# A 256 MB rotation by 90 degrees: the SBUF side of a DMA described as two runs of 8 KB instead of one of 16 KB

## The chip, the cores and the metric

The kernel runs on one core of one Trainium2 chip. The metric is device time in microseconds (us): 1260.99 us is the median of three runs before the change (1260.99 to 1261.13). The core has a tensor engine (PE), a vector engine (DVE), a scalar engine (ACT), GpSimd (POOL) and a sync engine (SP), and 16 DMA engines that move data between its on-chip memory (SBUF, 128 partitions) and the chip's main memory (DRAM).

## The reference

```python
def setup_inputs():
    return {"x": np.random.randn(8192, 8192).astype(np.float32), "k": 1}

def reference(x, k):
    return np.rot90(x, k)
```

With k = 1, `out[i, j] = x[j, 8191 - i]`: a transpose with the order of the columns reversed. Nothing is computed; 268 MB are read and 268 MB written.

## The kernel before

**Tiling.** The input is cut into 16 macros of 1024 rows (R) by 4096 columns (W). A macro comes in as 8 loads (T), each of 128 rows by 4096 columns: one row of 16 KB for each of the 128 partitions, 2 MB in all. It goes out as 8 stores (J), each of 512 input columns by 1024 input rows: 512 output rows of 1024 elements. In SBUF a store's buffer holds, for each partition, four output rows (G = 4) of 4 KB one behind the other, so 16 KB without a hole; in DRAM these four rows lie far apart. Two stores of the last macro are shaped otherwise: eight rows of 2 KB for each partition (END = 4 row blocks instead of 8).

**Stages.** There are 128 loads and 128 stores, 2 MB each.

1. SP issues load m into one of the landing buffers (LAND = 2 of them once the kernel runs; at the start the three output buffers take loads as well). It waits until the buffer's last load was read (`taken`, line 176).
2. DVE copies or transposes what landed into `ring` (line 337), an SBUF array that holds one macro. The slots that load m writes are those that output n = m - 8 was made from, so DVE first waits until output n is made (`s_pool` or `s_half`).
3. Output n is made in one of OUTS = 3 output buffers, either by PE (transposes into PSUM, line 376) with ACT copying from PSUM (line 415), or, for the outputs that DVE transposed in 32 by 32 blocks, by moves of these blocks on POOL (line 294, nine of sixteen), ACT (line 405, six) and DVE (line 319, one). In the macros between the first and the last ones, outputs 0 and 4 are made by PE and the other six by moves. Whoever writes an output buffer waits until the last store from it has landed (`room_for`, line 167).
4. ACT issues the store of output n (line 425).

So loads and stores hold each other: a load's rows can only go into `ring` when the output eight places before it is made, and an output can only be made when a store has given its buffer back.

**Queues.** Loads lie in SP's DMA queue (q1 in the profile), stores in ACT's (q10). Both run on the same 16 DMA engines. Each transfer has 128 partitions; each DMA engine takes eight of them.

**The place of the change.** `whole_reads` (line 37) goes through the finished program and rewrites the source pattern of some DMAs. A pattern is a list of (step, count) pairs, in elements, with the partitions first. The rewrite applies where the source has three such pairs, the last one contiguous, and the middle step as long as the last run:

- a load's source is `x[r0 + ..., c0 : c0 + W]`, which has two pairs, (8192, 128) and (1, 4096): the condition is not met;
- a store's source is the output buffer seen as `"m (g f) -> m g f"`: (4096, 128), (1024, 4), (1, 1024), or (4096, 128), (512, 8), (1, 512) for the two of the last macro. Here it is met, for all 128 stores.

Before the change it turns a store's source into (4096, 128), (1, 1), (1, 4096), one run of 16 KB for each partition. The destination stays as it was: four runs of 4 KB (or eight of 2 KB) for each partition.

Of the kernel before, what the change touches and what calls it, by code (L numbers as in the profile page):

```python
# [11 lines left out]
W = 4096  # L12
# [24 lines left out]
def whole_reads(nc):  # L37

    for fn in nc.m.functions:
        for block in fn.blocks:  # L40
            for n, ins in enumerate(block.instructions):
                if not isinstance(ins, mybir.InstDMACopy):
                    continue
                src = ins.ins[0]
                ap = [list(d) for d in src.ap]
                if len(ap) == 3 and ap[2][0] == 1 and ap[1][0] == ap[2][1]:
                    ap = [ap[0], [1, 1], [1, ap[1][1] * ap[2][1]]]
                    block.instructions[n] = copy.replace(
                        ins,
                        ins=[copy.replace(src, ap=ap)],  # L50
                        ant_dge_precooked=False,
                    )
# [7 lines left out]
def kernel(tc: tile.TileContext, x: bass.AP, k: bass.AP, out: bass.AP):  # L60
    nc = tc.nc
    assert k == 1, f"only k=1 supported, got {k}"
    nc.at_finalize(whole_reads)

    N, M = x.shape
# [400 lines left out]
```

## Time and profile before

| | before |
|---|---|
| median of three runs | 1260.99 us |
| the profiled execution, time | 1261.2 us |
| its span, first to last instruction | 1259.3 us |
| data moved | 537.22 MB, mean 427 GB/s |
| busy share of the span: PE, DVE, ACT, POOL | 26%, 49%, 54%, 64% |
| queue q1 (loads): records, share of 16 engines | 18432, 50.0% |
| queue q10 (stores): records, share of 16 engines | 18432, 50.1% |
| a load, median from issue to landing | 15.3 us |
| a store, median from issue to landing | 18.6 us |

The span is the time from the first to the last instruction of one profiled execution; the time of that execution is 1.9 us longer. Line numbers are those of the kernel above. "DMA" in a list of waits means that an instruction waited for a transfer to land. The trace also has one record for each DMA packet, with its queue, start, duration and bytes: 128 records of 16 KB and 16 of 4 bytes for each load and each store, the 4-byte ones being the increments of the semaphore, one on each engine. For a store the 16 KB are what is read from one partition in one run, whatever the runs on the DRAM side.

### The profile page before, as it was taken

What the parts mean: (1) busy time and instruction counts of PE and PEld (TensorE: products, weight loads), DVE (VectorE), ACT (ScalarE), POOL (GpSimd) and SP (SyncE); (2) the same over time, 40 slices, a digit from 0 to 9 for tenths busy, and PEclk for the clock granted to TensorE, in tenths of its full rate; (3) what the DMA queues carried; (4) which work ended last, traced back from release to release, by engine and by line L of the source; (5) the groups of instructions that cost most, each with busy time, mean ns of one, the idle gap of its engine ahead of it and who ended that gap; (6) DMA issues with size and microseconds to landing.
All of it is one profiled execution on the core that took longest, in us unless ns stands there. A gap on an engine that the chain in (4) does not pass through costs nothing.

```text
span 1259.3 us, 5455 instructions
## 1 busy us (share of the span) xinstructions
PE 326.2 (26%) x1556; PEld 265.3 (21%) x1556; DVE 618.3 (49%) x373; ACT 680.7 (54%) x636; POOL 809.8 (64%) x735
## 2 busy tenths in 40 slices
PE   1555111221123211222202222022221122214373
PEld 1444011211112110121201212012120121103373
DVE  3434654555545555555555555555545554454210
ACT  0344565565556655555555555556555665556464
POOL 0001886768867679676797767977678776795500
PEclk9986555555555555555555555556555565556687
DMA  9999999999999999999999999999999999999998
GB/s 398 413 429 431 428 428 430 429 431 429 429 430 429 430 428 429 430 429 431 428 429 432 426 430 429 429 431 428 431 430 428 430 429 429 429 428 429 431 423 372
DMA packets 36893, 537.22 MB, mean 427 GB/s; under 512 B 4096, under 2 KB 4096, under 8 KB 4096
## 3 DMA queue, kind: packets, MB, share of 16 engines
q10 hardware_dynamic: 18432, 268.44, 50.1%
q1 hardware_dynamic: 18432, 268.44, 50.0%
q8 instruction: 12, 0.20, 0.1%
q14 instruction: 17, 0.14, 0.0%
HBM read 268.44 MB, written 268.44 MB: 426 GB/s over the span
## 4 chain that ended last, share of the span: by engine, by line
DMA 49%; POOL 44%; ACT 3%; issue 2%; DVE 0%; PE 0%; ACTq 0%; POOLq 0%; SPq 0%; DVEq 0%
DMA out_dram<-buf 44%; POOL buf L294 44%; DMA buf<-in_x_dram 4%; ACT buf L415 3%; DVE ring L337 0%; PE ps L376 0%; ACTq L425 0%; POOLq L270 0%; SPq L256 0%; SPq L461 0%; DVEq L324 0%; SPq L118 0%
## 5 line engine op out<-in xcount | busy, mean ns | idle before, releaser
L294 POOL COPY buf<-ring 32x1024 f32<-32x1024 f32 (+1 forms) x729 | 809.1, 1110 | 379.8 <-DMA out_dram<-buf 349.8
L405 ACT COPY buf<-ring 32x1024 f32<-32x1024 f32 (+1 forms) x486 | 497.6, 1024 | 277.8 <-POOL buf L294 178.7
L376 PE MATMUL ps<-head,ring 128*128 128x128 f32 x1496 | 313.4, 381 | 914.1 <-DMA out_dram<-buf 419.2
L376 PEld LDWEIGHTS ps<-head,ring 128*128 128x128 f32 x1496 | 252.5, 198 | 974.8 <-DVE ring L337 430.2
L337 DVE COPY ring<-buf 128x1024 f32<-128x1024 f32 (+5 forms) x152 | 162.0, 1071 | 593.4 <-DMA buf<-in_x_dram 491.3
L337 DVE STREAM_TRANSPOSE ring<-buf 128x3072 f32<-128x3072 f32 (+2 forms) x125 | 357.8, 2871 | 0.0
L415 ACT COPY buf<-ps 128x2048 f32<-128x2048 f32 (+1 forms) x133 | 172.9, 1366 | 218.5 <-PE ps L376 145.4
L319 DVE COPY buf<-ring 32x1024 f32<-32x1024 f32 x81 | 108.1, 1334 | 0.0
L398 ACT COPY buf<-ps 128x512 f32<-128x512 f32 x15 | 8.8, 585 | 64.6 <-POOL buf L294 55.4
L362 PE MATMUL ps<-head,buf 128*128 128x128 f32 x60 | 15.9, 420 | 0.0
L362 PEld LDWEIGHTS ps<-head,buf 128*128 128x128 f32 x60 | 13.0, 229 | 0.0
L332 DVE COPY buf<-buf 128x512 f32<-128x512 f32 x15 | 6.4, 428 | 0.5
L389 ACT ACT_TABLE_LOAD x1 | 1.3, 1283 | 0.9 <-SPq L118 0.9
L274 POOL MEMSET head<- 128x128 f32 x1 | 0.2, 204 | 0.5 <-SPq L118 0.5
L276 POOL TENSOR_SCALAR_AFFINE_SELECT head<-head 128x128 f32<-128x128 f32 x1 | 0.3, 292 | 0.2 <-POOL head L274 0.2
L447 POOL MEMSET const-float32-0.0<- 128x1 f32 x1 | 0.1, 98 | 0.2 <-issue 0.2
L389 ACT COPY head<-head 128x1 f32<-128x1 f32 x1 | 0.2, 191 | 0.0
L447 POOL MEMSET const-uint8-127<- 128x1 uint8 x1 | 0.1, 102 | 0.0
L447 POOL MEMSET const-bfloat16-1.0<- 128x1 bf16 x1 | 0.1, 100 | 0.0
L447 POOL MEMSET const-float32-1.0<- 128x1 f32 x1 | 0.1, 98 | 0.0
## 6 DMA issues: line engine op xcount, KB each, us to landing
buf<-in_x_dram SPq DMA_DIRECT2D x128, 2048.0 KB, 15.3
out_dram<-buf ACTq DMA_DIRECT2D x128, 2048.0 KB, 18.6
```

What stands on the lines that cost most here:

```text
L276: e.affine_select(out=ident, in_=ident, compare_op=mybir.AluOpType.not_equal, fill=1.0, base=0, pattern=[[-1, P]], channel_multiplier=1,). ...
L294: i = e.tensor_copy(out=to, in_=of)
L319: i = e.tensor_copy(out=to, in_=of)
L332: e.tensor_copy(out=at(bufs[b][:], 0, [[CH, 1], [1, CH]]), in_=landed(b, js)).then_inc(s_rev, 1)
L337: turn(out=chunk(kk, t, js), in_=landed(b, js)).then_inc(s_rev, 1)
L362: i = e.transpose(corner[:, g * P : g * P + P], bufs[load_buf(m)][:, g * P : g * P + P], ident,)
L376: i = e.transpose(ps[h][:, to : to + P], chunk(kk, t, [j])[:, 0, off : off + P], ident,)
L389: e.copy(scratch, ident[:, :1])
L398: e.copy(at(bufs[b][:], rows - P, [[rows, G], [1, P]]), at(corner, 0, [[P, G], [1, P]]),).then_inc(s_freed, 1)
L405: i = e.copy(to, of)
L415: e.copy(at(bufs[b][:], cols[0], [[rows, deep], [1, run]]), at(ps[h][:], 0, [[run, deep], [1, run]]),).then_inc(s_ev, 1)
L447: nc = _bacc.Bacc("TRN2", target_bir_lowering=False, num_devices=1)
```

## The change

One line of `whole_reads` differs. A store's source pattern becomes (4096, 128), (2048, 2), (1, 2048): two runs of 8 KB for each partition instead of one of 16 KB. The bytes, their places, the destination pattern, the order of the instructions on every engine and all waits are the same. The title under which the change was made says "of a load"; in the program it is the stores that meet the condition, and a load is described as before: one run of 16 KB on either side.

```diff
                 src = ins.ins[0]
                 ap = [list(d) for d in src.ap]
                 if len(ap) == 3 and ap[2][0] == 1 and ap[1][0] == ap[2][1]:
-                    ap = [ap[0], [1, 1], [1, ap[1][1] * ap[2][1]]]
+                    ap = [ap[0], [W // 2, 2], [1, W // 2]]
                     block.instructions[n] = copy.replace(
                         ins,
                         ins=[copy.replace(src, ap=ap)],
```

## The prediction

> **What bounds the kernel now.** I read the page's DMA part first, then its queues and its waits, then a table of windows, and last the records of single DMA packets.
>
> ```profile
> DMA  9999999999999999999999999999999999999998
> GB/s 398 413 429 431 428 428 430 429 431 429 429 430 429 430 428 429 430 429 431 428 429 432 426 430 429 429 431 428 431 430 428 430 429 429 429 428 429 431 423 372
> DMA packets 36893, 537.22 MB, mean 427 GB/s; under 512 B 4096, under 2 KB 4096, under 8 KB 4096
> q10 hardware_dynamic: 18432, 268.44, 50.1%
> q1 hardware_dynamic: 18432, 268.44, 50.0%
> buf<-in_x_dram SPq DMA_DIRECT2D x128, 2048.0 KB, 15.3
> out_dram<-buf ACTq DMA_DIRECT2D x128, 2048.0 KB, 18.6
> ```
>
> The DMA engines are full in every slice, at 429 GB/s from the third slice on; loads and stores take half each, and their shares add to 100%. Nothing lies between 512 B and 8 KB: a store is recorded as 16 KB reads although it writes runs of 4 KB.
>
> ```profile
> DVE ring L337 <- DMA buf<-in_x_dram: 491.3, 106, 8.3
> PE ps L376 <- DMA out_dram<-buf: 419.2, 21, 29.7
> POOL buf L294 <- DMA out_dram<-buf: 349.8, 29, 120.6
> ```
>
> These waits (us in total, times, longest) all end with a transfer: the engines wait for DMA. The next table gives start and end, length, the busy time of five engines, the clock, DMA share and GB/s.
>
> ```profile
> 20.00:40.00 20.00, 4.28 (x15) 2.68 (x16) 9.42 (x5) 0.00 (x0) 0.00 (x0) 1.00 1.01 431
> 100.00:1150.00 1050.00, 227.69 (x953) 181.08 (x954) 555.84 (x340) 596.43 (x572) 784.32 (x710) 0.53 1.01 429
> 1215.00:1224.00 9.00, 7.78 (x68) 7.10 (x67) 0.00 (x0) 7.76 (x6) 0.00 (x0) 1.00 1.01 417
> 1230.00:1250.00 20.00, 9.28 (x81) 8.50 (x79) 0.00 (x0) 10.90 (x6) 0.00 (x0) 0.85 1.01 428
> ```
>
> Loads alone run at 431 GB/s, both at 429, stores alone at 428, the two stores of 2 KB runs at 417: the engines are as full in each, and the rate follows how a transfer is described.
>
> The packet records say how. Laid end to end they fall into 16 engines without holes; the time from a record's start to the next one's on its engine is the price of the record. It is 607 ns for 16 KB of a load, 612 to 613 ns for 16 KB of a store, 622 ns for 16 KB of the two stores with 2 KB runs, 6 ns for the 4 bytes of a semaphore. Each engine has 128 x 8 = 1024 load records, as many store records and 256 semaphore records: 1024 x 0.607 + 1024 x 0.6125 + 256 x 0.006 = 1250.3 us. The first record starts at 2.0 us and the last ends at 1257.4 us, which leaves 5.1 us for the slower first slices (398 and 413 GB/s) and small holes. The time is this sum, so the change is worth what it does to a store record, unless it leaves the DMA engines idle.
>
> **The change part by part.**
>
> *The loads* keep their pattern: 0.
>
> *The stores' reads.* 1024 records of 16 KB on each engine become 2048 of 8 KB. The trace has no store of that form, so I bound one added record. From below: 0. The prices 607, 612.5 and 622 ns for one, four and eight written runs rise by 1.8 ns a run at first and 2.4 later; if reading and writing went on beside each other and the slower counted, four written runs (some 5 ns over the load) could already cover one more read. A gain is excluded by the rows: no 16 KB record is cheaper than 607 ns, smaller runs were dearer each time, and two 8 KB pieces carry the same bytes. From above: the program's own fetches hold records of 8 KB, of 309 ns at least, against 611 ns for a load's 16 KB (these are durations, which overlap by 3 to 4 ns): 2 x 309 - 611 = 7 ns. In between: a 4-byte record takes 6 ns, almost no data, so about 5 ns is the price of a record as such. I take 4.8 ns, because that is a record more on the same queues and engines, while the 8 KB fetches belong to another queue. The sum: 1024 x 4.8 ns = 4.9 us; from below 0, from above 1024 x 7 ns = 7.2 us. There is no cover: the engines have no holes.
>
> The Trainium skill (DMA: Bandwidth & Descriptors, "Why small descriptors are slow") puts the fixed price of a packet inside a DMA engine at about 3 cycles; at the 850 MHz that its section "Where 436 GB/s comes from" gives, an estimate is 3.5 ns, and the sum would be 3.6 us, 1264.8 us. The 6 ns of the 4-byte record agree in size.
>
> *The issue* of a store on ACT takes 547 ns, that of a load 328 ns; more read descriptors may lengthen it, by no more than the same difference, I think: 0.2 us. It costs nothing while another store is still being moved: by issue times and semaphore records there is always at least one store in flight (one in 12% of the time, two in 78%, three in 10%). Without that cover it would be 128 x 0.22 = 28 us.
>
> *The turns.* While both queues hold work, an engine's records alternate, one load record, one store record. If a turn is a record, a store now moves 8 KB in a turn against a load's 16 KB, so stores get a third of the rate while a load is in flight, not half. Bytes do not change, and loads cannot run away: DVE takes load m only when output m - 8 is made. In a steady cycle of four outputs, 39.1 us, loads would be in flight for 4 x 4.9 x 1.5 = 29 us, with stores getting 9.8 us of work meanwhile and the other 9.8 us alone: it fits exactly, provided a store is always waiting. The DVE's 491 us of waiting for loads would turn into waiting for POOL and PE. I take 0 for this; its other end is the second rival.
>
> The Trainium skill (the same page, "Queues, rings and completion order") has an engine drain a whole packet of some 9 to 17 descriptors before it changes the queue; then the shares would stay as they are. The trace disagrees: the change comes after each record.
>
> Sum: the profiled execution's 1261.2 us (span 1259.3 and 1.9 around it) stands 0.2 us above the median, so 1261.0 + 4.9 = **1265.9 us**.
>
> **The rivals.**
>
> *1. The added read is hidden in the record (not slower).* Place: inside a DMA engine, where 16 KB of a store cost 612.5 ns because of four written runs, not of the read. For it: the step from four to eight runs (2.4 ns each) is larger than that from one to four (1.8), as it would be if the first written runs hid behind something. Against: the difference is a nanosecond. Price: 0 to 1 ns a pair, so 1261.0 to 1262.0, say 1261.5 us. It decides if a pair costs under 2.4 ns more. That the two adjoining runs are put together again on the way, so that the change does nothing, gives 1261.0 and is counted here.
>
> *2. Stores lose their turns and the DMA engines run dry (much slower).* Place: POOL's wait for a store, once in a 39.1 us cycle (longest normal wait 8 us). If loads are served first, then when POOL gets its buffer back only two stores are left, 9.8 us of work, while the next output takes nine moves, 10.4 us, plus 0.55 us of issue and about 1 us to the first record: up to 2.2 us idle in each of 29 cycles, 64 us, 1325 us at most; a quarter of it, as the loads that DVE releases fill most of it, gives 1282 us. For it: the alternation by records. Against: my count of the cycle keeps a store waiting throughout, if only by 1 to 2 us. It decides where there are moments with no store in flight.
>
> *3. Loads come earlier, and that helps (faster).* The same turns shorten a load's 15.3 us; DVE and PE wait less. But the DMA engines are full, and what can be won is the 5.1 us beside the sum, most of it in the first slices, before any store: I give it 3.5 us at most, 1257.5 us, and only if the added records cost nothing.
>
> **How the numbers follow.** A measurement of this kernel can tell about 0.2%, 2.5 us, from no change. The forecast (2.5 to 7 us more) has 0.48; hidden or undone, 0.29; run dry, 0.16; faster, 0.07. So slower 0.64, same 0.29, faster 0.07. The range: the lower end 1260.5 us takes in the first rival and leaves out the third; the upper end 1280 us takes in the upper bound of the record (1268.2) and the smaller half of the second rival, and leaves out about 0.09. The likeliest case alone has 1263.5 to 1268.2 us.
>
> **What would show it.** q10 should have 128 x (256 + 16) = 34816 records, q1 its 18432 still; if q10 has 18432, the runs were joined. Two store records should cost some 617 ns together, against 612.5: at that, stores alone near the end run at 424 or 425 instead of 428 GB/s, and the middle at 427 or 428 instead of 429. If the middle stays at 429, the first rival holds. If turns go by records, a load's median falls towards 9 to 12 us, a store's rises above 19 us, and DVE's wait for loads shrinks. If digits of the DMA row fall under 9, the second rival holds. The forecast is wrong if a pair costs under 2.4 ns or over 7 ns more, or if the engines show holes.

## The result and the profile after

The changed kernel takes 1276.6 us (median of six runs, 1274.11 to 1280.41) against 1261.04 us before (six runs): a ratio of 1.0126, 95% interval 1.0107 to 1.0145. It is slower, by 15.6 us: a small change, but well clear of the scatter. The profiled execution took 1280.4 us, span 1278.5 us, so it is one of the longer ones: 19.2 us over the profiled execution of before.

The DMA part of the page of the changed kernel, with the rate of each of 40 slices, the queues (records, MB, share of 16 engines) and the issues (KB each, median us from issue to landing):

```profile
DMA  9999999999999999999999999999999999999999
GB/s 398 423 428 428 429 423 426 404 425 412 408 430 408 428 426 407 418 397 430 428 420 430 412 429 426 425 430 426 425 427 420 432 419 427 426 431 428 397 421 381
DMA packets 53277, 537.22 MB, mean 420 GB/s; under 512 B 4096, under 2 KB 4096, under 8 KB 4096
q1 hardware_dynamic: 18432, 268.44, 50.1%
q10 hardware_dynamic: 34816, 268.44, 50.0%
buf<-in_x_dram SPq DMA_DIRECT2D x128, 2048.0 KB, 12.4
out_dram<-buf ACTq DMA_DIRECT2D x128, 2048.0 KB, 20.4
```

The stores' queue has the 34816 records that two runs of 8 KB make. Loads land sooner (12.4 us, 15.3 before), stores later (20.4, 18.6 before). And the rate is no longer even: before, it was 426 to 432 GB/s from the third slice to the thirty-eighth; now slices of 430 stand beside slices of 397 to 412. The DMA row says 9 throughout all the same. A record that takes twice its time counts as busy for all of it, so this row cannot show what was lost.

The waits of the changed kernel (us in total, times, longest):

```profile
DVE ring L337 <- POOL buf L294: 392.7, 67, 9.6
POOL buf L294 <- DMA out_dram<-buf: 368.7, 58, 121.5
DVE ring L337 <- DMA buf<-in_x_dram: 166.6, 46, 8.4
```

The kernel before had this line beside the ones in the prediction:

```profile
DVE ring L337 <- POOL buf L294: 98.9, 21, 6.4
```

DVE waited 491.3 us for loads before; now 166.6 us, and 392.7 us for POOL (98.9 before): loads now lie ready and wait for the output whose place they take. POOL waits for a store 58 times instead of 29. With the landing buffers full, SP often has no load to issue: between 60 and 1190 us no load was in flight for some 5% of the time (0% before).

Windows of the changed kernel: loads alone, the middle, one bad stretch in the middle, and stores alone near the end. Columns as in the prediction's table.

```profile
20.00:40.00 20.00, 4.14 (x15) 2.55 (x16) 9.56 (x5) 0.00 (x0) 0.00 (x0) 1.00 1.01 432
100.00:1150.00 1050.00, 223.24 (x940) 179.16 (x938) 520.07 (x335) 588.38 (x565) 757.96 (x702) 0.53 1.01 422
225.00:245.00 20.00, 7.81 (x34) 7.01 (x35) 13.36 (x7) 12.90 (x12) 18.32 (x18) 0.50 1.01 399
1250.00:1270.00 20.00, 7.46 (x64) 6.92 (x64) 0.00 (x0) 9.37 (x6) 0.00 (x0) 0.84 1.01 426
```

Loads alone run as before, stores alone at 426 GB/s against 428; the loss is in the middle, 422 against 429, where both queues meet, and there in stretches like the third line.

The packet records show what happens in such a stretch. I put them end to end on their engines as for the prediction; which engine a record ran on is inferred from its start and end. On one engine, from 225 us on (L a load record of 16 KB, S a store record of 8 KB, small letters the semaphores, in brackets the ns of a record that is longer than its kind):

```
S L S L s L L l S S S S S S S S S S S S S S S S s L(1058) L L L L L L L l S S S S S S S S S S S S S S S S(534) s L(1319) L(938) S L S L S L(629) S L(725) S L S L S l
```

A load's eight records and a store's eight used to alternate, with a share of one half each. Now a store needs sixteen turns and a load still eight, so the load is through when half of the store is left; the rest of the store runs by itself, and the next load may find an engine without any store. In this line its first record then takes 1058 or 1319 ns instead of 611. Some records after it are long too, even between two stores (629 and 725 ns at the end of the line).

Three figures sum this up for each kernel of this study; none needs to know which engine a record ran on. "One side" is the share of the time, from 60 us until shortly before the last load, in which at least 14 of the 16 engines were moving for the same queue. "Long" is the time, per engine, by which records exceeded the usual length of their kind, counted where it was over 50 ns. "Idle" is the time per engine without a record. "Records" is what the records' own prices come to against before, worked out from the prices below and 1024 pieces of 16 KB per queue and engine.

| kernel (load, store records) | median us | against before | one side | long us | idle us | records us |
|---|---|---|---|---|---|---|
| before (16 KB, 16 KB) | 1261.0 | | 9.5% | 2.7 | 2.0 | 0 |
| changed (16, 8) | 1276.6 | +15.6 | 48% | 18.2 | 4.2 | -0.5 |
| e1 (8, 8) | 1267.8 | +6.7 | 6% | 1.7 | 3.5 | +4.6 |
| e2 (8, 16) | 1283.0 | +21.9 | 49% | 12.2 | 9.3 | +5.1 |
| e3 (16, 4) | 1280.3 | +19.2 | 70% | 12.6 | 3.0 | +8.7 |
| e4 (4, 4) | 1284.1 | +23.0 | 2% | 1.3 | 1.5 | +23 |
| e5 (16, 8 and 16 by turns) | 1268.9 | +7.9 | 38% | 8.3 | 1.6 | -0.3 |
| e6 (16 written as 8, 16) | 1263.5 | +2.5 | 13% | 2.3 | 2.2 | +1.5 |
| e7 (16, 16, loads held) | 1327.5 | +66.5 | 47% | 46.9 | 23.7 | 0 |
| e8 (8, 4) | 1279.8 | +18.8 | 41% | 5.4 | 1.5 | +13.8 |

"One side", "long" and "idle" are of the profiled executions (1261.2 us before, 1280.4 us for the changed kernel, 1281.9, 1282.6, 1266.5 and 1326.4 us for e2, e3, e5 and e7). For the changed kernel 15.5 us more of long records and 2.2 us more idle account for 17.7 of its 19.2 us. In every run long records, idle time and the records' own price add up to the profiled difference to within 2 us.

The prices, from a record's start to the next one's on the same engine: 607 ns for 16 KB of a load, 612 to 613 ns for 16 KB of a store, 306 ns for 8 KB of either, 155 to 156 ns for 4 KB of either. So a store's pair costs 612 ns, no more than the one record that it replaces, as far as half a nanosecond can be told here.

### The profile page after: what moved, and what is told of

Same layout as the page of the kernel before. It is cut to its first block, busy times and chain, and to the rows that moved or that the text cites. A ratio compares the mean times of both kernels' runs of the same rounds, so it can differ in the third digit from the quotient of the medians.

```text
span 1278.5 us, 5455 instructions
## 1 busy us (share of the span) xinstructions
PE 323.1 (25%) x1556; PEld 265.3 (21%) x1556; DVE 589.1 (46%) x373; ACT 680.9 (53%) x636; POOL 790.2 (62%) x735
## 2 busy tenths in 40 slices
DMA packets 53277, 537.22 MB, mean 420 GB/s; under 512 B 4096, under 2 KB 4096, under 8 KB 4096
## 3 DMA queue, kind: packets, MB, share of 16 engines
q1 hardware_dynamic: 18432, 268.44, 50.1%
q10 hardware_dynamic: 34816, 268.44, 50.0%
## 4 chain that ended last, share of the span: by engine, by line
DMA 56%; POOL 30%; ACT 8%; issue 2%; DVE 1%; PE 1%; ACTq 1%; SPq 0%; DVEq 0%
DMA out_dram<-buf 52%; POOL buf L294 30%; ACT buf L415 7%; DMA buf<-in_x_dram 4%; DVE ring L337 1%; ACT buf L405 1%; PE ps L376 1%; ACTq L425 1%; SPq L256 0%; DVE buf L319 0%; ACT buf L398 0%; DVEq L324 0%; ACTq L163 0%; SPq L461 0%; SPq L118 0%
## 5 line engine op out<-in xcount | busy, mean ns | idle before, releaser
L294 POOL COPY buf<-ring 32x1024 f32<-32x1024 f32 (+1 forms) x729 | 789.5, 1083 | 417.4 <-DMA out_dram<-buf 368.7
L405 ACT COPY buf<-ring 32x1024 f32<-32x1024 f32 (+1 forms) x486 | 497.7, 1024 | 270.3 <-DMA out_dram<-buf 178.2
L337 DVE COPY ring<-buf 128x1024 f32<-128x1024 f32 (+5 forms) x152 | 150.2, 992 | 620.8 <-POOL buf L294 392.7
L337 DVE STREAM_TRANSPOSE ring<-buf 128x3072 f32<-128x3072 f32 (+2 forms) x125 | 358.2, 2873 | 0.0
L319 DVE COPY buf<-ring 32x1024 f32<-32x1024 f32 x81 | 90.3, 1115 | 18.7 <-DMA out_dram<-buf 18.7
L362 PEld LDWEIGHTS ps<-head,buf 128*128 128x128 f32 x60 | 12.6, 224 | 0.0
## 6 DMA issues: line engine op xcount, KB each, us to landing
buf<-in_x_dram SPq DMA_DIRECT2D x128, 2048.0 KB, 12.4
out_dram<-buf ACTq DMA_DIRECT2D x128, 2048.0 KB, 20.4
```

The source lines that it names most:

```text
L294: i = e.tensor_copy(out=to, in_=of)
L319: i = e.tensor_copy(out=to, in_=of)
L337: turn(out=chunk(kk, t, js), in_=landed(b, js)).then_inc(s_rev, 1)
L362: i = e.transpose(corner[:, g * P : g * P + P], bufs[load_buf(m)][:, g * P : g * P + P], ident,)
L405: i = e.copy(to, of)
```

## The experiments

The theory after the result: an engine changes the queue after each record; where the records differ in size, the queue with the larger ones gets ahead, each queue in turn leaves the engines to the other, and records grow long in these stretches (theory of turns). The rival: each added record costs what was lost, 15 ns (theory of records). All edits are against the kernel before.

**e1: loads in two runs as well.** The loads are read and also written in two runs.

```diff
+                if len(ap) == 2 and ap[1] == [1, W]:
+                    ap = [ap[0], [W // 2, 2], [1, W // 2]]
+                    to = [to[0], [W // 2, 2], [1, W // 2]]
                 ...
-                    ap = [ap[0], [1, 1], [1, ap[1][1] * ap[2][1]]]
+                    ap = [ap[0], [W // 2, 2], [1, W // 2]]
```

> Stores read in two runs of 8 KB as in the changed kernel, and loads in two runs of 8 KB too. Theory of turns (a queue's turn is one record, and unequal turns let one queue run dry): turns are equal again, both queues should stay occupied, no long records; a store's pair costs 612, a load's pair 612 instead of 607, so 1261 + 5 = 1266 us (1263 to 1268). Theory of records (each added record costs the 15.6 us / 1024 = 15 ns that the change lost): 1276.6 + 15.6 = 1292 us.

Measured: 1267.8 us, ratio 1.0055 (1.004 to 1.007). With 1024 more records on each engine than the changed kernel it is 8.8 us faster. Its rates by slice, its middle window and its issues:

```profile
GB/s 385 423 427 428 428 426 429 427 427 429 427 427 429 428 426 429 427 427 429 427 427 429 427 427 429 427 428 428 427 428 429 427 427 427 427 428 428 427 421 353
100.00:1150.00 1050.00, 224.80 (x950) 177.85 (x950) 546.82 (x340) 596.16 (x572) 779.13 (x706) 0.54 1.01 428
buf<-in_x_dram SPq DMA_DIRECT2D x128, 2048.0 KB, 15.5
out_dram<-buf ACTq DMA_DIRECT2D x128, 2048.0 KB, 18.7
```

Even slices again, and landings after 15.5 and 18.7 us, close to the 15.3 and 18.6 us of the kernel before. What is left is mainly the loads' own price: 612 against 607 ns, some 5 of the 6.7 us; another 1.5 us is idle time. The theory of records said 1292 us and is out.

**e2: loads in two runs, stores in one.** As e1, with the stores left as before the change.

> Loads in two runs of 8 KB, stores in one of 16 KB as before: the same number of records as in the changed kernel, on the other queue. Theory of records: 1276 us. Theory of turns: stores are now favoured two to one, loads always wait in their queue, stores run dry at times; a store record that starts after a pause was hardly longer than others in the changed kernel (26 ns against 84 for a load), so less is lost: 1265.8 us for the added load records and up to 6 more, 1264 to 1272 us.

Measured: 1283.0 us, ratio 1.0177 (1.016 to 1.0194): over both forecasts. Stores are favoured, as expected:

```profile
100.00:1150.00 1050.00, 223.32 (x907) 176.02 (x906) 541.03 (x341) 585.49 (x561) 753.61 (x703) 0.52 1.01 424
buf<-in_x_dram SPq DMA_DIRECT2D x128, 2048.0 KB, 15.3
out_dram<-buf ACTq DMA_DIRECT2D x128, 2048.0 KB, 12.2
```

A store lands after 12.2 us instead of 18.6. But my reason for a small loss fell. I had looked at which queue starts after a pause; but the stores, once through, leave the engines to the loads: 49% of the time on one side, 9.5 us more of long records, nearly all of them loads, and 7.3 us more idle.

**e3: stores in four runs of 4 KB.** In the changed line, `[W // 4, 4], [1, W // 4]`.

> Stores read in four runs of 4 KB, loads whole: turns of one to four. Theory of turns: more moments with an empty load queue than in the changed kernel (5.5% of the time there), a price of 4 x 155 = 621 ns against 612.5 for the records themselves (8.7 us), and at least the 15.6 us of the changed kernel for the runs dry: 1285 to 1300 us. Theory of records: 3 x 15.6 = 47 us more than before, 1308 us.

Measured: 1280.3 us, ratio 1.0149 (1.0127 to 1.0171), 5 us under the forecast. 70% of the time on one side, but 9.9 us more of long records, less than the changed kernel's 15.5. So the share of one-sided time does not by itself give the loss. A load lands after 10.8 us:

```profile
buf<-in_x_dram SPq DMA_DIRECT2D x128, 2048.0 KB, 10.8
```

**e4: both in four runs of 4 KB.** As e1, with 4 for 2.

> Stores and loads both in four runs of 4 KB: equal turns, and three records more than e3 for each 16 KB of a load. Theory of turns: no runs dry, only records: loads 621 against 607, stores 621 against 612.5, so 1261 + 14.3 + 8.7 = 1284 us, at or under e3 in spite of its 3072 more records on each engine. Theory of records: 6 x 15.6 = 94 us more than before, 1355 us.

Measured: 1284.1 us, ratio 1.0183 (1.0168 to 1.0198), the forecast 1284 us. In the middle it runs evenly at its own lower rate:

```profile
GB/s 379 421 421 421 422 420 421 421 421 421 421 421 422 421 421 421 421 422 422 420 422 421 421 421 422 421 422 421 421 422 422 421 421 421 421 421 422 421 421 375
```

So there is a price for many small records, 8 to 9 ns in 16 KB of a store read in four runs instead of one, and 14 ns in 16 KB of a load read and written in four instead of one, and it is quite apart from what the change lost.

**e5: every second store in two runs.**

```diff
+    stores = 0
                 ...
+                    stores += 1
+                    parts = 1 + stores % 2
-                    ap = [ap[0], [1, 1], [1, ap[1][1] * ap[2][1]]]
+                    ap = [ap[0], [W // parts if parts > 1 else 1, parts], [1, W // parts]]
```

> Every second store read in two runs of 8 KB, the others in one of 16 KB. Theory of turns: the load queue runs dry less often than the 5.5% of the changed kernel and the loss is at most half of its 15.6 us, 1263 to 1269 us; if a threshold has to be passed before queues run dry, nearer the lower end. Theory of records: half, 1269 us.

Measured: 1268.9 us (1266.5 to 1273.45), ratio 1.0067 (1.0044 to 1.0091): half of the change's loss. Both theories allowed for that, so the time alone does not tell them apart; the trace shows it as long records again, 5.6 us more than before in the profiled execution, which was 5.3 us longer.

**e6: loads read in one run, written in two.**

```diff
+                if len(ap) == 2 and ap[1] == [1, W]:
+                    ap = [ap[0], [1, 1], [1, W]]
+                    to = [to[0], [W // 2, 2], [1, W // 2]]
                 ...
```

> Loads read in one run of 16 KB as before, but written into SBUF in two runs of 8 KB; stores as before. If the turn and the record follow the runs that are read, q1 keeps its 18432 records, turns stay equal and nothing runs dry: 1261 to 1262.5 us. If a turn follows the runs that are written, this is as e2, 1283 us.

Measured: 1263.5 us, ratio 1.002 (1.001 to 1.0029). q1 keeps 18432 records, and nothing like e2 happens, so the turn follows the runs that are read:

```profile
q1 hardware_dynamic: 18432, 268.44, 49.9%
buf<-in_x_dram SPq DMA_DIRECT2D x128, 2048.0 KB, 15.4
out_dram<-buf ACTq DMA_DIRECT2D x128, 2048.0 KB, 18.3
```

The 2.5 us are 1 us over the forecast: a load's record costs 608 to 609 ns instead of 607, some 1.5 us.

**e7: the load queue made dry with all records as before.**

```diff
                     taken(e.wait_ge, last[-1])
+                    if 0 < m // T < KK - 1 and m % T in (2, 6):
+                        taken(e.wait_ge, m - 1)
```

> All records as before the change, turns equal, but twice in each of the 14 middle macros SP holds a load until both landing buffers have been read, so the load queue is dry and then gets two loads at once. If an empty load queue by itself costs (each of the 79 first records after a pause on each engine would stand for 15.6 / 79 = 0.2 us), 28 holds cost 6 us or more, 1267 us and up. If a pause costs only where stores have run out too, so that the engines start on loads alone, and stores go on here, under 3 us: 1261 to 1264 us.

Measured: 1327.5 us, ratio 1.0529 (1.0508 to 1.055). The premise of the second reading failed: the stores did not go on. By issue times and landings no store was in flight for 3.7% of the time (0.1% in the changed kernel), because outputs came late as well: DVE waited 697.2 us for loads, and POOL waited for DVE. Of the 200.8 us in the second line below, 125.5 are its first wait, which before was put down to a store (120.6 us); the rest, and the 167.0 us of the third line, are new. (The edit moves the lines after it down by two, so L339 is L337 of before; columns as in the other lists of waits.)

```profile
DVE ring L339 <- DMA buf<-in_x_dram: 697.2, 127, 15.0
POOL buf L294 <- DVE ring L339: 200.8, 14, 125.5
POOL buf L294 <- DVE buf L321: 167.0, 74, 4.9
```

The time is the sum of 44 us more of long records and 22 us more idle. So long records need neither small records nor unequal turns; holding the loads back is enough. And the trace shows one kind of start that is bad. Of the first load records of an engine after a pause of its load queue of over 1.5 us, in a moment when 11 to 16 engines had such a start within 0.3 us:

| | next record on the engine is a load | next is a store |
|---|---|---|
| e7 | 315 records, 539 ns too long | 14 records, 0 ns |
| changed | 154 records, 321 ns too long | 590 records, 0 ns |

(Means; the counts depend on the inferred engines and are good to about a tenth.) In the changed kernel, where one to three engines start thus, a load next means some 40 ns, where four to ten do, some 180 ns. So for these first records it is not the pause that costs but a start on many engines together with loads alone.

This explains only a part of the loss. By the table these starts hold 315 x 539 / 16 ns = 10.6 of the 45.9 us of long load records in e7 and 3.1 of 13.5 us in the changed kernel; in e2 all first load records after such a pause hold 0.2 of 11.8 us. And in the changed kernel the long load records do not lie mainly in the one-sided stretches. Sorted by what the engines do 0.1 us after the record's start (60 to 1190 us), 32.1 of 44.5 us in e7 and 6.9 of 10.0 us in e2 fall where at least 14 engines move for loads, but only 2.8 of 11.7 us in the changed kernel; there 8.8 us fall where neither queue has 14 engines. So the last part of the theory of turns, that records grow long in these stretches, is not shown for the changed kernel: unequal turns bring the long records, by a way that stays open.

**e8: two to one with smaller records.** Loads as in e1, stores in four runs of 4 KB.

> Loads in two runs of 8 KB, stores in four of 4 KB: the same ratio of two to one as in the changed kernel, with smaller records. Theory of turns: it is the ratio that counts, so all engines are again on one side in about half of the time and some 11 to 17 us go into long records, besides the records' own 4.9 + 8.7 us: 1286 to 1292 us, slower than e4 (1284 us), which has 2048 more records on each engine. If only the number of records and their size counted here, it would be 1261 + 13.6 = 1275 us.

Measured: 1279.8 us (1278.78 to 1285.62), ratio 1.0165 (1.0136 to 1.0194): between the forecasts, 5 us over the price of its records, and not slower than e4. The engines are on one side in 41% of the time, but the long records grow by 2.7 us only. So the forecast of the theory of turns failed here. The ratio of the turns sets how one-sided the engines are; how much that costs also depends on something else, which these runs do not settle.

**e9: the loads alone.** The stores, but for one at the end, and all compute are left out; this is the loop of loads.

```diff
+                for m in range(n_load):
+                    behind = 1 if m < n_load // 2 else 2
+                    if m >= behind:
+                        e.wait_ge(s_land[(m - behind) % NB], 16 * ((m - behind) // NB + 1))
+                    single(e, m)
```

> The 128 loads alone, all records 16 KB; the stores and everything between are left out, and the output is only one block. The first 64 loads are each issued when the one before has landed, the last 64 when the one before that has landed. If records grow long because all engines start on loads together with nothing else queued, the first records after each pause in the first half are long, by 500 ns in the mean as the 315 such records of e7, and the second half has none: 607 ns each. If it takes the change from stores to loads, the first half has no long records either, only pauses of some 2.5 us.

Measured in one profiled execution: 7.18 us from one load to the next in the first half, 4.86 us in the second. A window in each half (busy time of POOL, the only engine listed, then clock, DMA share and GB/s):

```profile
20.00:420.00 400.00, 0.00 (x0) 1.00 0.76 291
470.00:760.00 290.00, 0.00 (x0) 1.00 1.01 431
```

In the first half a load's first record on each engine takes 1173 ns in the mean (98% of them are long), the second 639, all others 610 or 611. In the second half, from 470 us on, they take 611 (one of 7632 is long). So a start of all engines on loads with nothing else queued costs 0.56 us on the first record without any store having been there, besides the pause itself; 2.3 us in all for each load. The kernel before shows it at its own start: the first record on each engine takes 1230 ns in the mean, while none of the 845 load records from 8 to 40 us, with loads alone but no pause, is long.

## Why the prediction came out as it did

The direction and the range were right (1276.6 us lies within 1260.5 to 1280), the likeliest figure, 1265.9 us, was not. The direction was right by luck: the term that made the forecast slower came to nothing, and the loss came by the turns, which the sum took as 0. Only the range, which was held open for half of the second rival, took this way in. The measured 15.6 us lies outside the forecast case (2.5 to 7 us, chance 0.48) and nearest to the rival that had 0.16.

- *The bound.* Right: the time followed the DMA engines in every run, and every difference is found, to within 2 us, in the records and the idle time of the engines.
- *The loads keep their pattern.* Right: 18432 records, 607 ns.
- *The stores' reads, 4.8 ns a record, 4.9 us.* This step failed. Two records of 8 KB cost 612 ns where one of 16 KB cost 612 to 613, so the term is -0.5 us, beside the lower bound of 0 and just below it. The first rival had the record right: a second read adds nothing. I took the price from the 4-byte record, and the same trace had the better row, the rise from one to four to eight written runs. That the written runs hide the read fits but is not shown: a load's pair costs 5 ns more in e1, but there the written side is split too, which by e6 has a price of 1 to 2 ns of its own; no run splits a load's read alone.
- *The issue.* 608 ns instead of 547 on ACT, less than the bound, and with no effect that the traces show.
- *The turns, taken as 0.* This step failed and holds nearly the whole loss (17.7 of the 19.2 us in the profiled execution). The mechanism stood there with its direction: turns by records, loads ahead, DVE waiting for POOL instead of loads. The count of the cycle was wrong in asking only that some store be in flight. In the changed kernel one nearly always is (99.9% of the time), yet an engine can be through with its own part of it, and the count did not ask whether a load is in flight at all (for some 5% of the time none was). I also priced a dry queue only as idle time. Idle grew by 2.2 us, long records by 15.5.
- *The second rival* (one quarter of its limit, 1282 us) came nearest, and the way of the loss was wrong: not engines that stand still, but engines whose records take longer. Its 1282 us are 1261 + 64 / 4 + 4.9 us of records (its upper end of 1325 us leaves the 4.9 us out); without the record term, which was not there, it gives 1277 us. That this meets the measured 1276.6 us is luck, as the quarter was a guess and idle time is 2.2 us of it. Nor was it decided where the rival said: moments with no store in flight make up 0.1% of the time. As the engines did not stand still, its sign, digits under 9 in the DMA row, did not show; the uneven GB/s row was the sign.
- *The third rival.* Loads did land earlier, by 2.9 us, and that won nothing.
- *The Trainium skill's 3 cycles a packet* (DMA: Bandwidth & Descriptors, "Why small descriptors are slow"), 3.5 ns by the estimate in the prediction: a store's pair shows none of it, a load's pair, read and written in two, 5 ns in e1. (The 1264.8 us beside it should be 1264.6 us on the base of the prediction's sum.) *The Trainium skill's rule that an engine drains 9 to 17 descriptors before it changes the queue* (the same page, "Queues, rings and completion order") is not what these traces show: e1 against the changed kernel, and e6 against e2, follow turns of one record that is read.

What stays open: why a load record is long when many engines start on loads together; what makes the larger part of the long load records long, those that are no such start and, in the changed kernel, mostly stand where both queues move; why some store records are long too (4.6 us in the changed kernel, 0.5 us in e2); and why the same ratio of turns costs 15.5 us of long records with 16 and 8 KB and 2.7 us with 8 and 4 KB.

## What to carry to other kernels

Where two queues share the DMA engines at full rate, look at the runs in which each is read: here the engine changed after each record, so the sizes set the shares, and equal sizes kept both queues going. At 8 KB splitting both sides cost less (6.7 us) than splitting either (15.6 and 21.9 us). At 4 KB it did not: the records' own price made both (23.0 us) dearer than the stores alone (19.2 us). Price a changed pattern by two terms, the record itself and the order in which queues run dry, and don't trust a busy row for the second: look at GB/s by slice and at the lengths of single records.

## What was not expected

A load record that starts on all engines at once, with nothing else queued, took 1173 ns instead of 611 (e9); in the changed kernel 590 first records of a start on many engines, with a store record next on the engine, were 0 ns too long in the mean. Splitting only the loads cost more (21.9 us) than splitting only the stores (15.6 us), 5.1 us of it in the records themselves. The read of a store of four written runs could be split in two at no price of its own, in four for 8 to 9 ns.
